# Where the operand rows of a split-float32 decoder trunk lie modulo 256 bytes

## The chip, the cores and the metric

The kernel runs on one core of a Trainium2 chip. The metric is device time in microseconds, the median of several runs. TensorE is called PE for matmuls and PEld for weight loads, VectorE DVE, ScalarE ACT, GpSimd POOL, and the queue that issues the weight transfers SP. SBUF is the on-chip memory that PE reads its operands from; each of its 128 partitions is a row of bytes, and "modulo 256" below speaks of a byte address within such a row.

## The reference, cut to what matters

A trunk of two layers over 256 tokens of width 1024, all in float32:

```python
for l in range(DEPTH):
    h = rms_norm(x, attn_norm[l])
    (c_val, c_gate, n_q, ..., d_q, d_k, d_v) = jnp.split(h @ w_in[l], splits, axis=-1)
    y_a = conv_module(c_val, c_gate, ...)     # gated causal depthwise convolution, 31 taps
    y_b = nsa_mixer(n_q, ...)                 # compressed, selected and windowed attention
    y_c = dilated_mixer(d_q, d_k, d_v, ...)   # three dilations, 12 heads
    x = x + jnp.concatenate([y_a, y_b, y_c], axis=-1) @ w_out[l]
    x = x + conv_ffn(rms_norm(x, ffn_norm[l]), w_up[l], ffn_dw[l], ffn_dw_b[l], w_down[l])
```

The feed-forward part is `u = causal_dwconv(h @ w_up)` (width 5632), then `(silu(gate) * value) @ w_down`.

## The kernel before

**Products of split numbers.** Each float32 operand of a weight product is kept as two rounded parts, hi and lo, and each product is three matmuls: hi by hi, hi by lo, lo by hi (`dense3`, lines 444 to 446). A matmul has a stationary operand of 128 columns, which PEld loads, and a moving operand, which streams through the array. While one matmul streams, the next one's stationary operand is loaded, so PE reads two rows of every partition at once.

**Two kinds of product.** In `feat_block` the weights are loaded and the activations move: 256 columns of `xT_hi` or `xT_lo`, with 128 columns of `whi` or `wlo` stationary. The feed-forward's `up` product (tile name `up`) and the two gated convolution chunks `c0` and `c1` (tile name `cv`) are of this kind. In `tok_chunk` and `proj` it is the other way round: 128 columns of the activations are loaded, and the weights move, 512 columns at a time (tiles `A` and `B` of the attention inputs, `oa` and `ob` of the output product, `da` and `db` of `down`), 384 (`Dq`, `Dk`, `Dv`) or 280 (the smaller chunk of `A`). The first two blocks of `up` in each layer also move the weights, 256 columns at a time (`up_head`, tile name `ut`): on the first of the two token tiles the matmuls with the lo part of the activations stand last (`dense_run`, lines 455, 456, 458), on the second they stand in threes (lines 444 to 446).

**The weight stream.** All weights come in pieces of 128 x 1024 numbers. SP loads a piece into `raw` (4 buffers), ACT writes its rounded part `whi` (line 209), DVE the rest `wlo` (line 212); there are 6 buffers of each and pieces are made 3 ahead of use (`take`, `slots`, `convert_piece`). One piece per layer, the third of `up` (`SPARE_UP`), lies in buffers of the attention stage instead (tile name `sp`).

**Order.** The program is written out in order, and the list `ORDER` interleaves the attention steps with the dilated chunks and the taps of the convolution. In an `up` block (48 matmuls) PE's result is scaled by ACT (line 1027), DVE adds the two other taps (line 222, four instructions), ACT takes the silu, DVE multiplies, and ACT and DVE split the result into `gT_hi` and `gT_lo`, beside two pieces of the weight stream.

**Where the tiles lie.** `cp` (constants and `xT`), `wp` (`raw`, `whi`, `wlo`) and `sp` (small tiles) are pools that lie behind one another in each partition's row; the attention's pool `mp` and the feed-forward's `fp` come behind them. Every slice that a dense product takes begins a whole number of 256 bytes behind its tile's start (the 280-column chunk, whose second half begins 96 bytes further, apart). So one number belongs to each kind of product: the stationary operand's address less the moving one's, modulo 256. The addresses are those which the built program of either kernel gives to its tiles.

| products | moving, stationary | columns | matmuls | distance before | after |
|---|---|---|---|---|---|
| `up` | `xT`, weights | 256 | 1920 | 192 | 64 |
| `cv` | `xT`, weights | 256 | 192 | 192 | 64 |
| `ut` | weights, `xT` | 256 | 192 | 64 | 64 (192 for the 48 that read `sp`) |
| `A`, `B` | weights, `xT` | 512 | 192 | 64 | 0 |
| `Dq`, `Dk`, `Dv` | weights, `xT` | 384 | 576 | 64 | 0 |
| `A`, small chunk | weights, `xT` | 280 | 96 | 64, 224 | 0, 160 |
| `oa`, `ob` | weights, `yT` | 512 | 192 | 192 | 0 |
| `da`, `db` | weights, `gT` | 512 | 528 | 192 | 0 |

Of the kernel before, what the change touches and what calls it, by code (L numbers as in the profile page):

```python
# [12 lines left out]
F32 = mybir.dt.float32  # L13
F32R = mybir.dt.float32r
# [5 lines left out]
P = 128  # L20
# [26 lines left out]
PIECE = 1024  # L47


def piece_list():  # L50
    out = []
    for l in range(L):
        first = ("a0", "a") if l == 0 else ("a", "a0")
        for name in first + tuple(n for n, _ in IN_CHUNKS[2:]):
            cols = CHUNKS[name]
            nk = 4 if len(cols) == 256 else 2
            for h in range(KT // nk):
                out.append((l, name, h, nk * len(cols)))
            if name == "a0":
                out += [(l, "w1", 0, PIECE), (l, "w1", 1, PIECE)]  # L60
        for i in range(KT):
            out.append((l, "out", i, PIECE))
        for f in range(NF):
            out += [(l, "up", 2 * f, PIECE), (l, "up", 2 * f + 1, PIECE)]
        for i in range(NF):
            out.append((l, "down", i, PIECE))
    return out


PIECES = piece_list()  # L70
# [86 lines left out]
W_BUFS = 6  # L157
# [3 lines left out]
SPARE_IN = ()  # L161
ORDER = "np(0) dq(0) t(6) np(1) dk(0) t(6) nf(0) np(2) dv(0) t(6) np(3) nf(1) da(0) dq(1) t(10) dk(1) t(100) ds(1) dv(1) ct(0) pv(1)"
TAIL = 4
CSC = (0,1)
TG = 2
STEP = 8
# [21 lines left out]
def tile_hybrid_trunk(ctx, tc, x_in, pos_in, stream, feats, gains, norms, const_in, out):  # L188
    nc = tc.nc

    cp = ctx.enter_context(tc.tile_pool(name="cp", bufs=1))
    wp = ctx.enter_context(tc.tile_pool(name="wp", bufs=3))
    sp = ctx.enter_context(tc.tile_pool(name="sp", bufs=2))
    ps = ctx.enter_context(tc.tile_pool(name="ps", bufs=1, space=bass.MemoryType.PSUM))

    def mm_bank(nm):
        return ps.tile([P, 512], F32, tag="mm", name=nm, bufs=3)
# [4 lines left out]
    def sc_bank(nm):  # L202
        return ps.tile([P, 1024], F32, tag="sc", name=nm, bufs=1)

    def o_bank(nm):
        return ps.tile([P, 512], F32, tag="o", name=nm, bufs=1)
# [55 lines left out]
    def slots(i):  # L262
        if i in state["spare"]:
            return state["spare"][i](i)
        return [wp.tile([P, PIECE], F32R, tag=t, name=f"{t}{i}", bufs=W_BUFS)[:, :] for t in ("whi", "wlo")]

    def emit_piece():
        i = state["next"]
# [26 lines left out]
    def take(name, ahead=AHEAD):  # L295
        i = cursor["i"]
        assert PIECES[i][1] == name, (PIECES[i], name)
        while state["next"] < min(len(PIECES), i + 1 + ahead):
            emit_piece()
        cursor["i"] += 1  # L300
        return emitted.pop(i)
# [19 lines left out]
    def norm_squares(t, nm, out, split=False):  # L321
        x = x_sb[t]
        ss = sp.tile([P, 2], F32, tag="ss", name=f"ss{nm}", bufs=2)
        for h in range(2):
            sl = slice(h * 512, h * 512 + 512)
            if split and h:
                nc.vector.tensor_tensor_reduce(out=out[:, sl], in0=x[:, sl], in1=x[:, sl], op0=ALU.mult, op1=ALU.add, scale=1.0, scalar=0.0,
                                               accum_out=ss[:, h:h + 1])
            else:
                nc.scalar.activation(out=out[:, sl], in_=x[:, sl], func=AF.Square, accum_out=ss[:, h:h + 1])  # L330
        return ss

    def norm_rms(ss, nm, eng=None):
        a = sp.tile([P, 1], F32, tag="na", name=f"na{nm}", bufs=2)
        ts(a, ss[:, 0:1], ss[:, 1:2], 1.0 / D, ALU.add, ALU.mult, eng=eng)
        ts(a, a, EPS, 1.0, ALU.add, ALU.mult, eng=eng)
        r = sp.tile([P, 1], F32, tag="nr", name=f"nr{nm}", bufs=2)
        rsqrt_into(r, a, [P, 1], nm, eng)
        return r

    def norm_tile(t, gi, nm, r=None):
        x = x_sb[t]
        g = gain_tiles[gi]
        xn = sp.tile([P, D], F32, tag="xn", name=f"xn{nm}", bufs=1)
        if r is None:
            r = norm_rms(norm_squares(t, nm, xn), nm)
        for h in range(2):
            sl = slice(h * 512, h * 512 + 512)
            scaled = stt(xn[:, sl], x[:, sl], r, g[:, sl], ALU.mult, ALU.mult)
            tp = tp_bank(f"tpx{nm}{h}")  # L350
            for k in range(4):
                nc.tensor.transpose(tp[:, k * P:(k + 1) * P], xn[:, h * 512 + k * P:h * 512 + (k + 1) * P], ident)
            tv = tp.rearrange("p (k c) -> p k c", k=4)
            hi = xT_hi[:, h * 4:h * 4 + 4, t * P:(t + 1) * P]
            lo = xT_lo[:, h * 4:h * 4 + 4, t * P:(t + 1) * P]
            ends = copy_act(hi, tv), tt(lo, tv, hi.bitcast(F32), ALU.subtract)
        return ends + (scaled,)
# [8 lines left out]
        )  # L366
    freq = cp.tile([P, 32], F32, name="freq")
    nc.gpsimd.dma_start(freq, const_in[:, CONST_N:CONST_N + 32])
    junk = wp.tile([P, PIECE], F32, tag="whi", name="junk", bufs=W_BUFS)
    ss0 = norm_squares(0, "a00", junk, split=True)  # L370
    x_ready = norm_tile(0, 0, "a00", norm_rms(ss0, "a00"))
    junk = wp.tile([P, PIECE], F32, tag="whi", name="junk1", bufs=W_BUFS)
    ss1 = norm_squares(1, "a01", junk)
    with tc.issue_after(x_ready[2].ins):
        emit_piece()
# [63 lines left out]
    nc.vector.memset(ones_m, 1.0 / 256.0)  # L439
    a_pad = cp.tile([P, 2, S + TAPS - 1], F32, name="a_pad")  # L440
    nc.vector.memset(a_pad, 0.0)

    def dense3(o, a_hi, a_lo, b_hi, b_lo, start, stop):
        nc.tensor.matmul(o, a_hi, b_hi, start=start, stop=False)  # L444
        nc.tensor.matmul(o, a_hi, b_lo, start=False, stop=False)  # L445
        nc.tensor.matmul(o, a_lo, b_hi, start=False, stop=stop)  # L446
# [41 lines left out]
    def feat_block(ws, bank):  # L488
        parts = [split_cols(w, 4) for w in ws]
        for h in range(2):  # L490
            for k in range(KT):
                hi, lo = parts[k // 4]
                sl = slice(h * P, (h + 1) * P)
                dense3(bank[:, h * S:(h + 1) * S], hi[:, k % 4, sl], lo[:, k % 4, sl], xT_hi[:, k, :], xT_lo[:, k, :], k == 0, k == KT - 1)

    for l in range(L):
        f = sp.tile([P, NPF], F32, tag="feat", name=f"feat{l}", bufs=1)
        ff = sp.tile([P, NFF], F32, tag="ffeat", name=f"ffeat{l}", bufs=1)
        ffp = ff.rearrange("p (f h k) -> p f h k", f=NF, h=2)
        c0 = 0  # L500
# [24 lines left out]
        def rope_tables():  # L525
# [3 lines left out]
            for q in Q_ORDER:  # L529
# [10 lines left out]
                ctab[q], stab[q] = c, s  # L540

        def rope(srcs, H, q, slots, nm, dup=False, np_=P):
            n = len(srcs)

# [150 lines left out]
        for b in range(2):  # L695
            ws = [take(f"c{b}") for _ in range(2)]
            bank = sc_bank(f"cv{l}{b}")[:, 0:512] if b in CSC else mm_bank(f"cv{l}{b}")
            feat_block(ws, bank)
# [254 lines left out]
        def proj(name, npieces, kts, a_hi, a_lo, acc, tail):  # L953
            def run(t, w, i, nhs=(0, 1)):
                hi, lo = w
                kk = kts[i]
                for nh in nhs:
                    sl = slice(nh * 512, nh * 512 + 512)
                    dense3(acc[t][nh], a_hi[:, kk, t * P:(t + 1) * P], a_lo[:, kk, t * P:(t + 1) * P], hi[:, sl], lo[:, sl],
                           i == 0, i == npieces - 1)  # L960

            for i in range(npieces - tail):
                w = take(name)
                for t in range(NT):
                    run(t, w, i)
            ws = [take(name) for _ in range(tail)]
            for t in range(NT):
                for nh in range(2):
                    for i in range(tail):
                        run(t, ws[i], npieces - tail + i, (nh,))  # L970
# [5 lines left out]
        obs = [[mm_bank(f"oa{l}{i}") for i in range(2)], [mm_bank(f"ob{l}0"), o_bank(f"ob{l}1")]]  # L976
        proj("out", KT, OUT_ORDER, yT_hi, yT_lo, obs, TAIL)
        for t in range(NT):
# [34 lines left out]
        def up_block(fb):  # L1013
            ws = [take("up") for _ in range(2)]
            bank = mm_bank(f"up{l}{fb}")
            feat_block(ws, bank)
            return bank

        NH = 2
        heads = up_head(NH)  # L1020
        for fb in range(NF):
            bank = heads[fb] if fb < NH else up_block(fb)
            u = fp.tile([P, 2, S], F32, tag="u", name=f"u{l}{fb}", bufs=3)
# [57 lines left out]
```

## Time and profile before

| | |
|---|---|
| median of 3 runs | 754.18 us (752.92 to 754.84) |
| the profiled execution | 753.01 us |
| its span | 751.2 us |
| PE busy | 733.9 us (98%) |
| PEld busy | 639.5 us |
| DVE busy | 597.3 us |
| ACT busy | 487.0 us |
| mean granted PE clock | 0.998 of full speed |
| read from HBM | 117.85 MB |

The busy time of PE is the time covered by at least one matmul record. Records overlap: a matmul's record is 276 to 280 ns long in the `up` stage, while the next one starts some 115 ns later. So what a matmul costs is read from the distance between starts, in the timeline, and not from the mean length of a record.

### The profile page before, as it was taken

How to read it: one execution, taken by the hardware profiler on the slowest of the kernel's cores; microseconds unless marked ns; L12 is line 12 of the kernel's file. 1: busy time of each engine (PE TensorE's matmuls, PEld its weight loads, DVE VectorE, ACT ScalarE, POOL GpSimd, SP SyncE). 2: the span in 40 equal slices, each digit the busy share in tenths (PEclk: the TensorE clock that was granted, in tenths of full speed). 3: DMA queues.
4: the chain of work that ended last, by engine and by line, in shares of the span. 5: the costliest groups of instructions: out<-in, count | busy, mean ns of one | idle time of the engine just before them, and what ended most of it. 6: DMA issues, size and time to landing. Idle time of an engine off the chain costs nothing.

```text
span 751.2 us, 13420 instructions
## 1 busy us (share of the span) xinstructions
PE 733.9 (98%) x4802; PEld 639.5 (85%) x4802; DVE 597.3 (80%) x1377; ACT 487.0 (65%) x1176; POOL 25.5 (3%) x67
## 2 busy tenths in 40 slices
PE   7999999999999999999999999999999999999997
PEld 5788777877999999988878977778789999999885
DVE  6889999886898888854487798989878888888441
ACT  4866998655676666643357589987538666666330
POOL 5200000000000000000040000000000000000000
PEclk9999999999999999999999999999999999999999
DMA  8753224344566555666456241335245656666631
GB/s 319 240 166 117 85 86 133 119 152 142 168 200 194 183 190 190 181 214 187 128 193 230 85 130 41 104 110 188 85 133 177 208 178 191 189 183 196 195 114 57
DMA packets 36005, 119.77 MB, mean 159 GB/s; under 512 B 4113, under 2 KB 4385, under 8 KB 35938
## 3 DMA queue, kind: packets, MB, share of 16 engines
q1 hardware_dynamic: 35714, 118.63, 49.7%
q8 instruction: 38, 0.62, 0.3%
q0 software_dynamic: 224, 0.28, 0.1%
q14 instruction: 29, 0.24, 0.1%
HBM read 117.85 MB, written 1.05 MB: 158 GB/s over the span
## 4 chain that ended last, share of the span: by engine, by line
PE 84%; DVE 6%; ACT 5%; DMA 2%; issue 2%; SPq 0%; DVEq 0%; POOL 0%; ACTq 0%
PE up L445 10%; PE up L444 10%; PE up L446 10%; PE da L444 3%; PE da L446 3%; PE da L445 3%; PE db L444 3%; PE db L446 3%; PE db L445 2%; DVE wlo L212 2%; DMA raw<-in_stream 2%; PE sc L745 1%; ACT whi L209 1%; PE Dk L444 1%; PE Dk L446 1%
## 5 line engine op out<-in xcount | busy, mean ns | idle before, releaser
L212 DVE TENSOR_TENSOR wlo<-raw,whi 128x1024 fp32r<-128x1024 f32 (+3 forms) x232 | 260.3, 1127 | 88.2 <-ACT whi L209 87.3
L209 ACT ACTIVATE whi<-raw 128x1024 fp32r<-128x1024 f32 (+3 forms) x232 | 224.7, 978 | 107.9 <-PE db L446 54.6
L445 PE MATMUL up<-xT_lo,whi 128*128 128x256 f32 x640 | 179.2, 280 | 0.0
L444 PE MATMUL up<-xT_hi,whi 128*128 128x256 f32 x640 | 178.7, 279 | 0.0
L446 PE MATMUL up<-xT_hi,wlo 128*128 128x256 f32 x640 | 178.6, 279 | 0.0
L444 PEld LDWEIGHTS up<-xT_hi,whi 128*128 128x128 f32 x640 | 120.3, 188 | 0.0
L445 PEld LDWEIGHTS up<-xT_lo,whi 128*128 128x128 f32 x640 | 120.1, 188 | 0.0
L446 PEld LDWEIGHTS up<-xT_hi,wlo 128*128 128x128 f32 x640 | 119.7, 187 | 0.0
L222 DVE SCALAR_TENSOR_TENSOR u<-up,ffeat,u 128x255 f32<-128x255 f32 (+1 forms) x176 | 80.0, 478 | 2.6
L222 DVE SCALAR_TENSOR_TENSOR acc<-a_pad,dwh,acc 128x256 f32<-128x256 f32 x120 | 54.2, 480 | 0.3 <-ACT acc L709 0.2
L1034 ACT ACTIVATE sl<-u 128x256 f32<-128x256 f32 x44 | 18.1, 415 | 47.7 <-DVE u L222 47.7
L1027 ACT ACTIVATE u<-up,ffeat 128x256 f32<-128x256 f32 x88 | 44.2, 552 | 0.0
L444 PE MATMUL db<-whi,gT_hi 128*128 128x512 f32 x88 | 34.7, 394 | 0.0
L444 PE MATMUL da<-whi,gT_hi 128*128 128x512 f32 x88 | 34.7, 394 | 0.0
L446 PE MATMUL db<-whi,gT_lo 128*128 128x512 f32 x88 | 34.5, 392 | 0.0
L446 PE MATMUL da<-whi,gT_lo 128*128 128x512 f32 x88 | 34.5, 392 | 0.0
L445 PE MATMUL da<-wlo,gT_hi 128*128 128x512 f32 x88 | 34.2, 388 | 0.0
L445 PE MATMUL db<-wlo,gT_hi 128*128 128x512 f32 x88 | 34.1, 388 | 0.0
L209 ACT ACTIVATE ms<-ms,dd 128x128 f32<-128x128 f32 (+1 forms) x64 | 24.2, 447 | 0.0
L444 PE MATMUL A<-whi,xT_hi 128*128 128x280 f32 (+1 forms) x64 | 23.4, 366 | 0.5 <-ACT xT_hi L209 0.5
L446 PE MATMUL A<-whi,xT_lo 128*128 128x280 f32 (+1 forms) x64 | 22.9, 359 | 0.3 <-DVE xT_lo L212 0.3
L444 PE MATMUL Dq<-whi,xT_hi 128*128 128x384 f32 x64 | 23.0, 359 | 0.0
(348 smaller groups left out, 1573.0 us busy)
## 6 DMA issues: line engine op xcount, KB each, us to landing
raw<-in_stream SPq DMA_DIRECT2D x172, 512.0 KB, 4.2
raw<-in_stream SPq DMA_DIRECT2D x48, 384.0 KB, 3.2
raw<-in_stream SPq DMA_DIRECT2D x8, 280.0 KB, 4.4
w<-in_stream SPq DMA_DIRECT2D x4, 512.0 KB, 5.3
gain<-in_norms SPq DMA_DIRECT2D x3, 512.0 KB, 3.6
x<-in_x SPq DMA_DIRECT2D x4, 256.0 KB, 3.8
out<-x SPq DMA_DIRECT2D x4, 256.0 KB, 2.0
feat<-in_feats SPq DMA_DIRECT2D x2, 339.0 KB, 4.1
```

The source lines that it names most:

```text
L209: return nc.scalar.activation(out=o, in_=i, func=AF.Copy, **kw)
L212: return nc.vector.tensor_tensor(out=o, in0=a, in1=b, op=op)
L222: return nc.vector.scalar_tensor_tensor(out=o, in0=a, scalar=s, in1=b, op0=op0, op1=op1)
L444: nc.tensor.matmul(o, a_hi, b_hi, start=start, stop=False)
L445: nc.tensor.matmul(o, a_hi, b_lo, start=False, stop=False)
L446: nc.tensor.matmul(o, a_lo, b_hi, start=False, stop=stop)
L745: nc.tensor.matmul(sc[:, j * 512:j * 512 + n], QT[hp_, pair, P:2 * P], keys[hp_], start=True, stop=True)
L1027: nc.scalar.activation(out=u[:, h], in_=z, func=AF.Identity, scale=c[:, 2:3], bias=c[:, 3:4])
L1034: nc.scalar.activation(out=sl_, in_=u[:, 0], func=AF.Silu)
```

## The change

The tiles `whi` and `wlo` become 64 numbers (256 bytes) wider, and `slots` gives out 1024 of their columns from a start that depends on the piece: 64 bytes in for `c0`, `c1` and `up`, 192 bytes in for the four pieces of `up` that `up_head` reads (the one in the spare buffers keeps its place there), at the start for all others. Two tiles of 64 bytes, `gap_cp` and `gap_sp`, are put at the end of two pools; they move the pools behind them, so `raw`, `whi` and `wlo` start at 128 modulo 256 in place of 64, and the tiles of `mp` and `fp` (`yT`, `gT` and all else there) lie 128 bytes further. `xT_hi` and `xT_lo` stay at 128. The constant `NH` moves from the function to the top of the file.

```diff
+NH = 2
...
-        return [wp.tile([P, PIECE], F32R, tag=t, name=f"{t}{i}", bufs=W_BUFS)[:, :] for t in ("whi", "wlo")]
+        _, name, h, _ = PIECES[i]
+        at = 16 if name in ("c0", "c1", "up") else 0
+        if name == "up" and h < 2 * NH:
+            at = 48
+        return [wp.tile([P, PIECE + 64], F32R, tag=t, name=f"{t}{i}", bufs=W_BUFS)[:, at:at + PIECE] for t in ("whi", "wlo")]
...
-    junk = wp.tile([P, PIECE], F32, tag="whi", name="junk", bufs=W_BUFS)
+    junk = wp.tile([P, PIECE + 64], F32, tag="whi", name="junk", bufs=W_BUFS)
...
+    for pool in (cp, sp):
+        gap = pool.tile([P, 16], F32, name=f"gap_{pool.name}", bufs=1)
+        nc.vector.memset(gap, 0.0)
```

On all five engines the instructions stand in the same order as before, but for two on DVE. Its first rows before, ahead of the first norm (`junk` holds the squares, `ssa` their sums):

```order
L242 MEMSET one_row 1x128
L439 MEMSET ones_m 128x128
L441 MEMSET a_pad 128x572
L327 ISA junk,ssa_103<-x_67 128x512
L327 ISA ssa_103 128x1
```

and in the changed kernel:

```order
L243 MEMSET one_row 1x128
L444 MEMSET ones_m 128x128
L446 MEMSET a_pad 128x572
L449 MEMSET gap_cp 128x16
L449 MEMSET gap_sp 128x16
L332 ISA junk,ssa_103<-x_67 128x512
```

The two small clears stand between the clear of `a_pad` and the first norm's sum; nothing else moved.

## Rows read from the trace of the kernel before

**Rows 1.** The page, busy us, share of the span and instructions of each engine.

```profile
span 751.2 us, 13420 instructions
...
PE 733.9 (98%) x4802; PEld 639.5 (85%) x4802; DVE 597.3 (80%) x1377; ACT 487.0 (65%) x1176; POOL 25.5 (3%) x67
```

**Rows 2.** The page, the chain that ended last, by engine and line.

```profile
PE 84%; DVE 6%; ACT 5%; DMA 2%; issue 2%; SPq 0%; DVEq 0%; POOL 0%; ACTq 0%
PE up L445 10%; PE up L444 10%; PE up L446 10%; PE da L444 3%; PE da L446 3%; PE da L445 3%; PE db L444 3%; PE db L446 3%; PE db L445 2%; DVE wlo L212 2%; DMA raw<-in_stream 2%; PE sc L745 1%; ACT whi L209 1%; PE Dk L444 1%; PE Dk L446 1%
```

**Rows 3.** Stretches: PE, PEld, DVE, ACT, POOL busy us, clock, DMA share, GB/s.

```profile
60.00:80.00 20.00, 19.66 (x128) 16.54 (x128) 19.89 (x71) 13.83 (x40) 0.00 (x0) 1.00 0.27 81
...
215.00:315.00 100.00, 100.00 (x851) 100.00 (x850) 87.20 (x145) 66.16 (x108) 0.00 (x0) 1.00 0.60 189
```

**Rows 4.** Timeline of PE, up block: start us, us, instruction; 41 starts apart.

```profile
207.12 0.28 PE L444 MATMUL up<-xT_hi,whi 128*128 128x256 f32 x1
...
211.94 0.28 PE L446 MATMUL up<-xT_hi,wlo 128*128 128x256 f32 x1
```

**Rows 5.** Timeline of PE, ut, second token tile, first layer; 44 starts apart.

```profile
196.56 0.28 PE L444 MATMUL ut<-whi,xT_hi 128*128 128x256 f32 x1
...
201.55 0.28 PE L446 MATMUL ut<-whi,xT_lo 128*128 128x256 f32 x1
```

**Rows 6.** Timeline of PE, ut, first token tile, first layer; 9 starts apart.

```profile
189.87 0.28 PE L455 MATMUL ut<-whi,xT_hi 128*128 128x256 f32 x1
...
190.93 0.28 PE L456 MATMUL ut<-wlo,xT_hi 128*128 128x256 f32 x1
```

**Rows 7.** Timeline of PE, ut, first token tile, second layer; 9 starts apart.

```profile
559.36 0.28 PE L455 MATMUL ut<-whi,xT_hi 128*128 128x256 f32 x1
...
560.38 0.28 PE L456 MATMUL ut<-wlo,xT_hi 128*128 128x256 f32 x1
```

**Rows 8.** Timeline of PE, ut, second token tile, second layer; 39 starts apart.

```profile
566.64 0.28 PE L446 MATMUL ut<-whi,xT_lo 128*128 128x256 f32 x1
...
571.06 0.28 PE L446 MATMUL ut<-whi,xT_lo 128*128 128x256 f32 x1
```

**Rows 9.** Timeline of PE, attention input B, 512 columns; 12 starts apart.

```profile
38.64 0.40 PE L444 MATMUL B<-whi,xT_hi 128*128 128x512 f32 x1
...
41.44 0.40 PE L444 MATMUL B<-whi,xT_hi 128*128 128x512 f32 x1
```

**Rows 10.** Timeline of PE, down product, 512 columns; 12 starts apart.

```profile
338.28 0.39 PE L444 MATMUL da<-whi,gT_hi 128*128 128x512 f32 x1
...
341.03 0.39 PE L444 MATMUL da<-whi,gT_hi 128*128 128x512 f32 x1
```

**Rows 11.** Timeline of PE, dilated chunk Dk, 384 columns; 21 starts apart.

```profile
84.22 0.34 PE L444 MATMUL Dk<-whi,xT_hi 128*128 128x384 f32 x1
...
87.93 0.34 PE L444 MATMUL Dk<-whi,xT_hi 128*128 128x384 f32 x1
```

**Rows 12.** Who waited for whom, DVE and ACT, 215 to 315 us: us, times, longest.

```profile
DVE wlo L212 <- ACT whi L209: 9.9, 17, 0.6
...
ACT whi L209 <- PE up L445: 8.4, 17, 1.3
```

**Rows 13.** DVE lines 222 and 439: min/median/max ns, first and last start us, forms.

```profile
L222 DVE SCALAR_TENSOR_TENSOR acc<-a_pad,dwh,acc x120: 473/479/486, 61.5 to 510.6; 128x256 f32<-128x256 f32 x120
...
L439 DVE MEMSET ones_m<- x1: 165/165/165, 1.0 to 1.0; 128x128 f32 x1
```

**Rows 14.** Timeline of DVE, the program's start: clears, then the first norm.

```profile
1.20 0.54 DVE L441 MEMSET a_pad<- 128x572 f32 x1
4.42 0.69 DVE L327 CUSTOM_DVE_ANT_0 junk<-x 128x512 f32<-128x512 f32 x1 [2.69 <-DMA x<-in_x]
```

**Rows 15.** Groups of PE instructions by line and shape: xcount | busy us, mean ns.

```profile
L444 PE MATMUL up<-xT_hi,whi 128*128 128x256 f32 x640 | 178.7, 279 | 0.0
...
L444 PE MATMUL cv<-xT_hi,whi 128*128 128x256 f32 x64 | 18.2, 284 | 0.0
```

More of the change, by code (lines that the diff above doesn't have):

```diff
@@ L368, in tile_hybrid_trunk @@
     nc.gpsimd.dma_start(freq, const_in[:, CONST_N:CONST_N + 32])
-    junk = wp.tile([P, PIECE], F32, tag="whi", name="junk", bufs=W_BUFS)
+    junk = wp.tile([P, PIECE + 64], F32, tag="whi", name="junk", bufs=W_BUFS)
     ss0 = norm_squares(0, "a00", junk, split=True)
     x_ready = norm_tile(0, 0, "a00", norm_rms(ss0, "a00"))
-    junk = wp.tile([P, PIECE], F32, tag="whi", name="junk1", bufs=W_BUFS)
+    junk = wp.tile([P, PIECE + 64], F32, tag="whi", name="junk1", bufs=W_BUFS)
     ss1 = norm_squares(1, "a01", junk)
@@ L1017, in up_block @@
             return bank
-        NH = 2
         heads = up_head(NH)
```

## The prediction

> **What bounds the kernel now.** I read the page first: PE is busy for 733.9 of 751.2 us and no other engine comes near [rows 1]. The chain that ended last goes by PE for 84% of the span, and its three largest entries are the lines of the `up` product, 10% each [rows 2]. In the stretch of `up` from 215 to 315 us PE is covered all the time at a granted clock of 1.00 (the 2.4 GHz level), DVE is busy for 87.20 and ACT for 66.16 of 100 us [rows 3]. So in `up` only the pace of the matmuls counts. Busy time can't show that pace, since records overlap, so the next view is the timeline, and in it the distance between starts.
>
> In `up` 41 starts take 211.94 - 207.12 = 4.82 us, 117.6 ns each [rows 4]. At 2.4 GHz 256 columns would be 106.7 ns, so each matmul loses 10.9 ns although nothing waits. The heads `ut` have the same shape, 256 columns moving against 128 stationary, with the two operands' roles exchanged, and there 44 starts take 4.99 us, 113.4 ns each [rows 5]. What differs is the table's last but one column: distance 192 in `up`, 64 in `ut`. That is the pair of rows that bears on the change.
>
> It isn't clean, and the reader should see that too. On the first token tile `ut` also has distance 64. In the second layer it runs at 1.02 us for 9 starts, 113.3 ns [rows 7], in the first layer at 1.06 us for 9, 117.8 ns [rows 6]. On the second tile of the second layer it is fast again, 4.42 us for 39 starts, 113.3 ns [rows 8]. So distance 64 allows the fast pace and doesn't force it: the stream of loads and the stream of columns settle in one of two rhythms. Of four stretches at distance 64 three are fast; at distance 192 I find the slow one alone.
>
> **The change, part by part.**
>
> *`up`, 192 to 64.* 3 x 640 = 1920 matmuls [rows 15]. If they take the rhythm of [rows 5], each gains 117.6 - 113.4 = 4.2 ns: 1920 x 4.2 = 8.1 us. All of it is on the path, because PE is the only engine in the chain there. The bounds are 0 (rhythm of [rows 6]) and 8.1; I take 8.1, because `up` runs in threes without a break, as [rows 5, 8] do, and those are the nearest rows.
>
> What is late next? A block has 48 matmuls: 48 x 117.6 = 5.64 us now, 5.44 after. DVE needs 87.2% of 5.64, which is 4.92 us, and still fits. Its waits in `up`, 9.9 us in 100, end with ACT's `whi`, and ACT's own wait for a free buffer, 8.4 us, ends with PE [rows 12]; so both shrink when PE is quicker. The transfers use 0.60 of the DMA engines there [rows 3] and would use 0.62.
>
> *`cv`, 192 to 64.* 192 matmuls (three lines of 64 [rows 15]) by 4.2 ns is 0.8 us. DVE is busy for 19.89 of 20 us from 60 to 80 us, where part of them lies [rows 3], so I count half, 0.4 us; the ends are 0 and 0.8.
>
> *Weights that move, to distance 0.* No dense product of the trace has distance 0, so this part is bounded by other rows. 512 columns cost 2.75 us for 12 starts, 229.2 ns, at distance 192 [rows 10], and 2.80 us for 12, 233.3 ns, at distance 64 [rows 9]. The lowest pace seen, 113.4 ns for 256 columns, would be 226.8 ns for 512. For `oa`, `ob`, `da`, `db`, 720 matmuls, the ends are 720 x (226.8 - 229.2) = -1.7 us and 720 x (233.3 - 229.2) = +3.0 us; I take 0, the middle of the three levels. For `A` and `B`, 192 matmuls, the ends are 192 x (226.8 - 233.3) = -1.2 us and one more step of 4.1 ns, +0.8 us; at the middle level they gain 192 x 4.1 = 0.8 us, and I count half, -0.4, as these stages also wait for weights and for ACT. For the 576 matmuls of `Dq`, `Dk`, `Dv`, 3.71 us for 21 starts is 176.7 ns [rows 11]; 1.5 times 113.4 is 170.1, so the ends are 576 x -6.6 = -3.8 us and 576 x 4.1 = +2.4 us. DVE and ACT share the path there, so I take -0.4 us. The 96 matmuls of 280 columns and the 48 of `ut` that read the spare buffers (distance 192, at most +0.2 us) I leave at 0.
>
> *The other engines' operands.* DVE now reads `raw` and `whi` 64 bytes apart where they lay level. The taps of the convolution read `a_pad` at a start that moves by 4 bytes from tap to tap against `acc`; all 120 lie between 473 and 486 ns [rows 13], so I count 0. Were the split of a piece 1% longer, DVE would still have room in `up` by the sum above. ACT and the transfers get no new work, and I count 0.
>
> *The two clears.* 165 ns would be the price of a clear eight times as wide [rows 13]. DVE waits 2.69 us for the first input after its last clear [rows 14], which hides both: 0. Without that cover they would cost 0.3 us.
>
> **Sum.** -8.1 - 0.4 - 0.4 - 0.4 = -9.3 us. The profiled execution took 753.01 us, so one like it would take 743.7 us; it lies 1.2 us under the median of 754.18, and from the median the sum gives **744.9 us**. Each gain is set against the path and I expect none of it to come back in a later stage: `down` is bound by PE as well.
>
> **Rivals.**
>
> *One rhythm of two.* `up` settles in the fast rhythm in one layer and in the slow one in the other, as the first tile of `ut` did [rows 6, 7], or DVE falls behind here and there and gives part of the gain back. Half of `up` remains: 744.9 + 4.1 = 749.0 us. For it: one of four stretches at distance 64 is slow. Against it: in threes, both stretches were fast [rows 5, 8], and a block of `up` doesn't wait for anything that would restart the rhythm.
>
> *The distance has no part in it.* The slow stretch at distance 64 [rows 6] shows that something else sets the rhythm too; if it sets it alone, `up` keeps 117.6 ns and the time is 754 us within a microsecond or two. Against it stands that `up`, 1920 matmuls long, never fell into the fast rhythm. The Trainium skill, "TensorE: Matmul & The Clock Gate", section "Step-by-step: what each phase is for", says that PE has two independent read ports on SBUF, one for the streamed operand and one for the weight load, and that loading the next weights takes no read bandwidth from the running matmul. By that rule the place of the operands could not matter and this rival would hold; by the rows it does matter, since equal shapes run at 113.4 and 117.6 ns.
>
> *Level is the worst place.* The moving weights and the loaded activations now start on the same 256-byte position, and if reads of both rows at once are what costs, level could cost most. The price is in the 720 matmuls of `oa` to `db`, on the path in full: the level of [rows 9] gives +3.0 us, another step in `A`, `B` +0.8, and up to +2.4 in the dilated chunks, 6.2 us together. With the gain of `up` this still leaves 753 us; without it, 760.4 us. It ends on the slower side if `up` gains nothing and the 720 matmuls lose over 3.2 ns each (2.3 us). For it: distance 64 is good at 256 columns and worse than 192 at 512, so the order of places isn't the same for all lengths. Against it: nothing in the trace at distance 0.
>
> **How the numbers follow.** About 0.3%, 2.3 us, is what a measurement of this kernel can tell from no change. Chances: forecast 0.66 (739 to 751 us with the ends of the moving weights), one rhythm of two 0.16 (about 746 to 752), no effect 0.10 (754), level the worst with no gain in `up` 0.08 (757 to 761). The low end of the range is the forecast with all ends on their good side: a further 1.7 + 0.8 + 3.4 + 0.4 = 6.3 us off, 738.6, taken as 739, since not all of the dilated chunks lies on the path. The high end, 752, is one layer's gain with +3.0 us in the 720. Faster by over 0.3% (under 751.9): 0.66 + 0.15 = 0.81; slower: 0.08; within: 0.11.
>
> **What would show it.** Right: starts in `up` 113.4 ns apart, some 880 matmuls in a stretch of 100 us where now there are 851, PE still covered all the time. Starts in `down` between 226.8 and 233.3 ns tell which end holds for level operands; `Dk` between 170 and 181. Wrong: `up` at 117.6 in either layer, a PE that waits for `wlo` in `up`, or `down` beyond 233.3 ns.

## The result, and the profile after

The changed kernel takes **747.24 us**, the median of 20 executions (742.98 to 752.31), against 753.97 us of the kernel before beside it (20 executions, 752.78 to 756.04). The ratio is 0.9907 with a 95% interval of 0.9889 to 0.9926. So it is faster by 0.9%, the sign and the range hold, and the time lies 2.3 us above the forecast of 744.9.

The spread says more than the median. The executions of the kernel before lie within 3.3 us, those of the changed kernel fall into groups: four from 742.98 to 743.38, one at 745.46, twelve from 746.25 to 748.05, three from 751.58 to 752.31. The steps are some 4 us wide, which is what one layer of `up` was worth in the forecast. The granted clock doesn't make the groups: of the fifteen executions with a mean clock of 0.999 or 1.0, four take 742.98 to 743.38, ten 746.62 to 748.05 and one 751.58.

The profiled execution took 752.31 us. Its page, the busy times and the largest entries of the chain (lines have moved: the three matmuls of a dense product are now 452 to 454, the two halves of a split 210 and 213):

```profile
span 750.5 us, 13422 instructions
...
PE 730.9 (97%) x4802; PEld 637.0 (85%) x4802; DVE 597.2 (80%) x1379; ACT 486.9 (65%) x1176; POOL 25.6 (3%) x67
...
PE 84%; DVE 8%; ACT 4%; issue 2%; DMA 2%; SPq 0%; DVEq 0%; ACTq 0%
```

These read like [rows 1, 2]; PE is still the engine that the chain runs through. The difference is in the distance between starts. The timeline of PE, `up` in the first layer, then in the second, 41 starts apart each:

```profile
209.83 0.28 PE L452 MATMUL up<-xT_hi,whi 128*128 128x256 f32 x1
...
214.66 0.28 PE L454 MATMUL up<-xT_hi,wlo 128*128 128x256 f32 x1
...
584.74 0.28 PE L452 MATMUL up<-xT_hi,whi 128*128 128x256 f32 x1
...
589.39 0.28 PE L454 MATMUL up<-xT_hi,wlo 128*128 128x256 f32 x1
```

The first layer needs 4.83 us, 117.8 ns a matmul, as before [rows 4]. The second needs 4.65 us, 113.4 ns, as forecast; over a whole layer the paces are 117.8 and 113.3 ns. Neither changes along the way: from the first dozen starts of a layer to its last block the pace is one of these two. The stretches show the same (PE, PEld, DVE, ACT, POOL busy us, clock, DMA share, GB/s; the row that answers to [rows 3] first, one of the second layer behind it):

```profile
215.00:315.00 100.00, 100.00 (x851) 100.00 (x850) 86.98 (x145) 67.42 (x108) 0.00 (x0) 1.00 0.60 189
...
580.00:680.00 100.00, 100.00 (x885) 100.00 (x884) 90.94 (x153) 70.40 (x114) 0.00 (x0) 1.00 0.63 197
```

851 matmuls in 100 us as before, then 885. PE is covered throughout in both, and DVE rises to 90.94 and still fits.

The moving weights, now level with the activations: `da` (512 columns, 12 starts apart), `B` (512, 12) and `Dk` (384, 17):

```profile
329.79 0.39 PE L453 MATMUL da<-wlo,gT_hi 128*128 128x512 f32 x1
...
332.51 0.39 PE L453 MATMUL da<-wlo,gT_hi 128*128 128x512 f32 x1
```

```profile
41.23 0.39 PE L452 MATMUL B<-whi,xT_hi 128*128 128x512 f32 x1
...
43.96 0.39 PE L452 MATMUL B<-whi,xT_hi 128*128 128x512 f32 x1
```

```profile
87.04 0.33 PE L452 MATMUL Dk<-whi,xT_hi 128*128 128x384 f32 x1
...
89.98 0.33 PE L454 MATMUL Dk<-whi,xT_lo 128*128 128x384 f32 x1
```

`da` takes 226.7 ns a matmul (229.2 in [rows 10]), `B` 227.5 (233.3 in [rows 9]), `Dk` some 173 (176.7 in [rows 11]). The two clears, in the timeline of DVE:

```profile
1.69 0.07 DVE L449 MEMSET gap_cp<- 128x16 f32 x1
1.71 0.07 DVE L449 MEMSET gap_sp<- 128x16 f32 x1
4.41 0.69 DVE L332 CUSTOM_DVE_ANT_0 junk<-x 128x512 f32<-128x512 f32 x1 [2.62 <-DMA x<-in_x]
```

They take 0.07 us each and DVE waits for its input for 2.62 us behind them.

**Why this one execution took 752 us.** With one fast layer it should belong to the 747 group. It lost some 5 us elsewhere: 3.2 us ahead of the first `up` and 2.1 us ahead of the second, against the profile of `after_again` below. Part of that is lost in the first 17 us, at a clock of 1.00: there the first `gain` matmuls start 1.2 us later and the later products of `A` 1.7 us later. The greater part is lost where the granted clock falls, once ahead of each `up`. Stretches of 2 us:

```profile
34.00:36.00 2.00, 0.77 (x5) 0.37 (x4) 1.45 (x4) 1.94 (x5) 1.58 (x4) 1.00 0.89 274
36.00:38.00 2.00, 2.00 (x10) 1.54 (x10) 2.00 (x5) 1.40 (x4) 0.00 (x0) 0.64 0.66 238
38.00:40.00 2.00, 2.00 (x6) 1.61 (x5) 1.10 (x8) 0.64 (x2) 0.00 (x0) 0.50 0.73 244
```

PE is covered for 0.77 of 2 us, a pause inside the product `A` ahead of the small matmuls of `cmp`, and then the granted clock is 0.50 for a while, the 1.2 GHz level. The same pattern stands at 524 to 532 us, behind two shorter pauses. In the profile of `after_again` PE pauses as long and the clock stays:

```profile
32.00:34.00 2.00, 0.77 (x5) 0.28 (x4) 1.50 (x4) 1.95 (x4) 1.94 (x4) 1.00 0.76 223
34.00:36.00 2.00, 2.00 (x11) 1.47 (x12) 2.00 (x4) 1.39 (x4) 0.00 (x0) 1.00 0.69 233
```

What the fall costs is the way from the first matmul of `cmp` to the first of `B`, in the profiled execution and then in `after_again`:

```profile
35.32 0.27 PE L674 MATMUL cmp<-feat,hk 64*32 64x64 f32 x2 [1.23 <-issue]
...
41.23 0.39 PE L452 MATMUL B<-whi,xT_hi 128*128 128x512 f32 x1
```

```profile
33.67 0.27 PE L674 MATMUL cmp<-feat,hk 64*32 64x64 f32 x2 [1.23 <-issue]
...
37.98 0.39 PE L452 MATMUL B<-whi,xT_hi 128*128 128x512 f32 x1
```

That is 5.91 against 4.31 us, so the fall costs 1.6 us here; the one at 528 us costs 1.6 us too, by the same comparison. Such a fall happens in some executions and not in others of the same program, so it isn't set by where the operands lie. The rest is the late start (1.7 us) and 0.5 us at 524 us.

### The profile page after: what moved, and what is told of

Same layout as the page of the kernel before. It is cut to its first block, busy times and chain, and to the rows that moved or that the text cites. A ratio compares the mean times of both kernels' runs of the same rounds, so it can differ in the third digit from the quotient of the medians.

```text
span 750.5 us, 13422 instructions
## 1 busy us (share of the span) xinstructions
PE 730.9 (97%) x4802; PEld 637.0 (85%) x4802; DVE 597.2 (80%) x1379; ACT 486.9 (65%) x1176; POOL 25.6 (3%) x67
## 4 chain that ended last, share of the span: by engine, by line
PE 84%; DVE 8%; ACT 4%; issue 2%; DMA 2%; SPq 0%; DVEq 0%; ACTq 0%
PE up L454 10%; PE up L452 10%; PE up L453 10%; PE da L453 3%; PE da L452 3%; PE da L454 3%; PE db L452 2%; PE db L453 2%; PE db L454 2%; DVE wlo L213 2%; PE sc L753 1%; PE Dk L452 1%; PE Dk L454 1%; PE Dk L453 1%; DMA raw<-in_stream 1%
## 5 line engine op out<-in xcount | busy, mean ns | idle before, releaser
L213 DVE TENSOR_TENSOR wlo<-raw,whi 128x1024 fp32r<-128x1024 f32 (+3 forms) x232 | 260.1, 1126 | 83.1 <-ACT whi L210 82.0
L453 PE MATMUL A<-wlo,xT_hi 128*128 128x280 f32 (+1 forms) x64 | 23.2, 366 | 0.0
```

The source lines that it names most:

```text
L213: return nc.vector.tensor_tensor(out=o, in0=a, in1=b, op=op)
```

## The experiments

Theory: distance decides the pace, and at 64 `up` settles in one of two rhythms when a layer enters it. Rivals: distance has no part; or the whole gain came from the level placement of the moving weights.

**One part alone.** `up_alone` gives the kernel before the distance of 64 in `up` and `cv`, and leaves the moving products at 64 and 192. Against the kernel before (its buffers start 64 bytes further down than those after the change, hence other numbers):

```diff
+        _, name, h, _ = PIECES[i]
+        at = 32 if name in ("c0", "c1", "up") else 0
+        if name == "up" and h < 2 * NH:
+            at = 0
+        return [wp.tile([P, PIECE + 64], F32R, tag=t, name=f"{t}{i}", bufs=W_BUFS)[:, at:at + PIECE] for t in ("whi", "wlo")]
```

> The changed placement for the up and cv products alone: their weights lie 64 bytes behind the activations (distance 64), all other products keep the distances of the kernel before (A, B, Dq, Dk, Dv at 64, oa to db at 192). Theory, two rhythms: each layer's up settles once, at its first matmuls, at 113.4 or at 117.8 ns a start and keeps that to its end, so the times fall into three groups, near 753, 749 and 745 us, and down stays at 229.2 ns. Rival, the distance has no part in it: up at 117.8 ns in both layers of every execution, 754 us within a microsecond. Rival, the gain of the whole change came from the moving weights: no group under 752 us.

`level_alone` does the other half: the changed kernel, with `up` and `cv` back at distance 192.

```diff
-        at = 16 if name in ("c0", "c1", "up") else 0
+        at = 48 if name in ("c0", "c1", "up") else 0
```

> The changed placement for the moving weights alone: A, B, Dq, Dk, Dv, oa to db at distance 0 as in the changed kernel, up and cv at distance 192 as in the kernel before. Theory: up at 117.8 ns a start in every execution, down at 226.7 ns against 229.2, so 720 matmuls gain 2.5 ns each, 1.8 us, and with A and B some 2.5 us in all: 751.5 us in one narrow group. Rival, the spread of the changed kernel comes from the moving weights: times here spread over 8 us as well.

`after_again` is the changed kernel once more beside these two.

> The changed kernel once more, nothing else edited, for a second profile beside a second time. Theory, two rhythms: in each layer all blocks of up run at 113.4 or all at 117.8 ns, and the layer's choice need not be that of the first profile (117.8 in the first layer, 113.3 in the second); an execution with one fast layer takes 747 us, with two 743, with none 751. Rival, the first layer is always slow because of what lies before it: 117.8 there again.

| kernel | median us | all executions | ratio to before, 95% |
|---|---|---|---|
| before | 753.43 | 752.48 to 755.45 | |
| `up_alone` | 749.44 | 745.15, 748.67, 749.04, 749.44, 749.74, 750.0, 752.29 | 0.9937 (0.9913 to 0.996) |
| `level_alone` | 751.78 | 751.27 to 755.31 (12, ten of them up to 753.4) | 0.9981 (0.9969 to 0.9993) |
| `after_again` | 742.86 | 742.21, 742.72, 742.99, 743.85 | 0.9854 (0.9837 to 0.9871) |

Stretches of the two layers of `up`, and 12 starts of the down product, first in `up_alone`:

```profile
215.00:315.00 100.00, 100.00 (x851) 100.00 (x851) 87.29 (x145) 66.51 (x107) 0.00 (x0) 1.00 0.60 190
580.00:680.00 100.00, 100.00 (x884) 100.00 (x884) 90.91 (x151) 69.41 (x113) 0.00 (x0) 1.00 0.65 198
...
329.74 0.39 PE L449 MATMUL db<-whi,gT_hi 128*128 128x512 f32 x1
...
332.49 0.39 PE L449 MATMUL db<-whi,gT_hi 128*128 128x512 f32 x1
```

and in `level_alone`:

```profile
215.00:315.00 100.00, 100.00 (x851) 100.00 (x850) 87.15 (x146) 66.15 (x108) 0.00 (x0) 1.00 0.61 188
580.00:680.00 100.00, 100.00 (x851) 100.00 (x851) 87.59 (x146) 66.53 (x109) 0.00 (x0) 1.00 0.63 191
...
329.72 0.39 PE L452 MATMUL da<-whi,gT_hi 128*128 128x512 f32 x1
...
332.44 0.39 PE L452 MATMUL da<-whi,gT_hi 128*128 128x512 f32 x1
```

At distance 64 one layer is fast (884 starts in 100 us) and one is not; at 192 neither is. The moving weights gain on their own: 2.72 us against 2.75 us for 12 starts, 226.7 against 229.2 ns, and 1.65 us of the time. So neither rival holds for the whole: without level weights the median still falls by 4.0 us, and without distance 64 it falls by 1.65 us. The times of `up_alone` fall as expected around 745 (one) and 749 us (five); the seventh, 752.29, has a mean clock of 0.994, so its time doesn't tell its group.

In `after_again` both layers are fast, 41 starts in 4.64 and 4.65 us:

```profile
209.84 0.28 PE L452 MATMUL up<-xT_hi,whi 128*128 128x256 f32 x1
...
214.48 0.28 PE L454 MATMUL up<-xT_hi,wlo 128*128 128x256 f32 x1
...
584.75 0.28 PE L453 MATMUL up<-xT_lo,whi 128*128 128x256 f32 x1
...
589.40 0.28 PE L452 MATMUL up<-xT_hi,whi 128*128 128x256 f32 x1
```

The same program as in the profile above, in another execution: the program alone doesn't fix the rhythm of a layer. The stage table takes the first start of each stage from the three traces:

| stage, us | before | after, profiled | `after_again` |
|---|---|---|---|
| to the first `up` | 201.7 | 204.0 | 200.8 |
| `up`, first layer | 114.6 | 114.6 | 110.4 |
| down, first layer | 60.4 | 59.9 | 59.9 |
| to the second `up` | 194.4 | 196.8 | 194.7 |
| `up`, second layer | 114.6 | 110.4 | 110.4 |
| down and the end | 65.4 | 64.8 | 64.8 |
| span | 751.2 | 750.5 | 740.9 |

**All distances in one program.** `sweep` gives every block of `up` another distance, eight of them in steps of 32 bytes, in another order in each layer; pieces of the down product and the dilated chunks get theirs too.

```diff
+        turn = (0, 5, 2, 7, 4, 1, 6, 3) if l == 0 else (6, 4, 2, 0, 7, 5, 3, 1)
...
+        if name == "up":
+            at = 48 if h < 2 * NH else 8 * turn[(h // 2 - NH) % 8]
+        elif name == "down":
+            at = 8 * turn[h % 8]
+        elif name[0] == "d":
+            at = 8 * turn[(2 * h + l) % 8 if name[2] == "0" else (2 * h + 1 - l) % 8]
```

> Distances swept inside one execution: from the third block of up on, each block takes one of the eight distances 0, 32 to 224, in one order in the first layer and another in the second; the pieces of down and of the dilated chunks run through the same eight. Only the starts are of interest, not the total time. Theory: the pace of a block changes at its border with the distance; 192 is always at 117.8 ns, 64 at either pace, and if some distance is at 113.4 in both layers and after different neighbours, that is a place that leaves no choice. For 512 columns 0 is at 226.7, 64 near 233.3, 192 near 229.2. Rival, the pace is set by something else than the distance: no change at the borders, one pace through the layer.

It took 753.66 us. A block has 48 matmuls, so the first start of one block to that of the next is its pace. Blocks at 0, 160 and 64 in the first layer (one row for each block's start), the block at 192 there, and a block at 192 in the second layer:

```profile
247.65 0.29 PE L457 MATMUL up<-xT_hi,whi 128*128 128x256 f32 x1
...
253.41 0.28 PE L457 MATMUL up<-xT_hi,whi 128*128 128x256 f32 x1
...
259.16 0.28 PE L457 MATMUL up<-xT_hi,whi 128*128 128x256 f32 x1
...
264.60 0.28 PE L457 MATMUL up<-xT_hi,whi 128*128 128x256 f32 x1
...
281.56 0.28 PE L457 MATMUL up<-xT_hi,whi 128*128 128x256 f32 x1
...
287.01 0.28 PE L457 MATMUL up<-xT_hi,whi 128*128 128x256 f32 x1
...
617.87 0.28 PE L457 MATMUL up<-xT_hi,whi 128*128 128x256 f32 x1
...
623.52 0.28 PE L457 MATMUL up<-xT_hi,whi 128*128 128x256 f32 x1
```

5.76, 5.75 and 5.44 us for 0, 160 and 64, which is 120.0, 119.8 and 113.3 ns; 5.45 us (113.5 ns) for 192 in the first layer and 5.65 us (117.7 ns) in the second. The pace of all distances, ns a matmul, from the starts in the later part of each block:

| distance | 0 | 32 | 64 | 96 | 128 | 160 | 192 | 224 |
|---|---|---|---|---|---|---|---|---|
| `up`, 256 columns | 120.0 | 118.4 | 113.3 | 117.3 | 118.7 | 119.9 | 113.3 or 117.8 | 116.6 |
| down, 512 columns | 226.7 | 232.7 | 233 to 234 | 233 to 234 | 232 | 233 to 234 | 229 | 233 to 234 |

For 384 columns the longest unbroken stretches give 174 to 175 ns at 0, 173 to 174 at 192 and 173 to 177 at the others, too close together to name a best. So the place alone moves `up` by 5.9% within one program, which the rival without distance doesn't allow; the best place for 256 columns is not the best for 512; and 0, with 160 the worst of these eight for `up`, is the best for the down product. One thing was not expected: 192 ran at 113.3 ns in the first layer, so it knows the fast rhythm too. In the order of the kernel before it was never met: none of the 68 executions of that kernel on record is under 752.14 us, and none of the twelve of `level_alone` under 751.27.

Is it the distance, or the place of one operand alone? For 512 columns the rows tell. Distance 192 gave 229 ns with weights at 64 modulo 256 and `gT` at 0 [rows 10] and with weights at 192 and `gT` at 128 (`sweep`); distance 64 gave 233.3 with weights at 64 and `xT` at 128 [rows 9] and 233 to 234 with weights at 192 and `gT` at 128 (`sweep`). Equal distances have equal paces although the places differ. For `up` no run can tell: `xT` lies at 128 in all of them, so the distance and the weights' own place change together.

By the rule of two independent ports in the Trainium skill, "TensorE: Matmul & The Clock Gate", section "Step-by-step: what each phase is for", all blocks would last equally long; the measured 113.3 to 120.0 ns decide against drawing that from it.

**Both rhythms at one distance.** `sweep_seeds` pairs the blocks: first one at a seed distance, then one at 64 (first layer) or 192 (second).

```diff
+            seed = (0, 8, 24, 32, 40, 56, 4, 28, 12, 52)[f // 2 % 10]
+            at = 48 if f < 0 else seed if f % 2 == 0 else 48 if l else 16
```

> Ten seeds, one to each pair of blocks of up: the first block of a pair takes distance 0, 32, 96, 128, 160, 224, 16, 112, 48, 208, the second 64 in the first layer and 192 in the second. Only starts count. Theory, a border chooses between two rhythms by the phase that the block ahead leaves: behind one seed the choice is always the same, and 64 and 192 both know 113.3 and 117.8 ns; behind 128 and 160, 64 runs at 113.3. Rival, 64 forces the fast rhythm and only its first entry behind the transposes fails: every block at 64 at 113.3, every block at 192 at 117.8.

It took 750.29 us. The first starts around two blocks at 64, the first behind one at 32, the second behind one at 96:

```profile
219.67 0.28 PE L454 MATMUL up<-xT_hi,whi 128*128 128x256 f32 x1
...
225.33 0.28 PE L454 MATMUL up<-xT_hi,whi 128*128 128x256 f32 x1
...
230.96 0.28 PE L454 MATMUL up<-xT_hi,whi 128*128 128x256 f32 x1
...
236.41 0.28 PE L454 MATMUL up<-xT_hi,whi 128*128 128x256 f32 x1
```

5.66 us and 5.45 us for the same 48 matmuls at the same distance. At 64 the fast rhythm came behind 48, 96, 128, 160, 208 and 224, the slow one behind 0, 16, 32 and 112. At 192 it is another list: fast behind 0 and 32, slow behind the other eight. So both distances know both rhythms, and a layer can change its rhythm where the distance changes. The distance of the block ahead doesn't settle which one follows: behind 32, 192 is fast here and in the first layer of `sweep`, and slow in the second layer of `sweep`.

**Forcing the rhythm: a miss.** In `seeded` the first block of a layer behind the heads lies at 128, behind which 64 had been fast every time. `seeded_sp` also gives the piece in the spare buffers, which `ut` reads, distance 64 in place of 192 (the last two lines of the diff).

```diff
+        elif name == "up" and h < 2 * NH + 2:
+            at = 32
...
-                mp.tile([P, 3, 3, P], F32, tag="pT", name=f"sp{i}{u}", bufs=4).rearrange("p a b c -> p (a b c)")[:, :PIECE].bitcast(F32R) for u in range(2)]
+                mp.tile([P, 3, 3, P], F32, tag="pT", name=f"sp{i}{u}", bufs=4).rearrange("p a b c -> p (a b c)")[:, 32:32 + PIECE].bitcast(F32R) for u in range(2)]
```

> The changed kernel with one edit: the third block of up in each layer, the first that feat_block makes, takes distance 128 in place of 64; all later blocks stay at 64. In the sweep every block at 64 that came behind one at 160 or 128 ran at 113.3 ns. Theory, the first matmuls choose the rhythm and a border chooses it anew: that block runs at 118.8 ns and all 19 later ones at 113.3 in both layers of every execution; one narrow group of times near 743.5 us (the fast group, 743.0, plus 96 matmuls at 5.4 ns, 0.5 us). Rival, the rhythm drifts or flips by itself in the course of a layer: a spread from 743 to 752 us as with the changed kernel.

> The kernel before this one, and the spare buffers' piece of up begins 128 bytes further in its tile, so that the 48 matmuls of ut that read it have distance 64 like the other 144. Theory: ut no longer drops to 117.8 ns at its second block; at most 96 matmuls gain 4.4 ns, 0.4 us, against seeded; 743.1 us, not to be told from seeded in a few runs. Rival, the first norm's transposes and not ut set the pace there: the same time to 0.1 us.

`seeded`: 743.8, 743.81, 745.73, 748.4, 749.37, 750.5, median 747.06, ratio 0.99 (0.987 to 0.993). `seeded_sp`: 745.52, 745.81, 748.71, 749.21, 751.05, 751.9, median 748.96, ratio 0.9932 (0.9905 to 0.9959). In both profiles all blocks at 64 are fast in both layers, and still the times spread as before, from 743.8 to 748.7 us at a mean clock of 0.999 or more. So a seed that worked in one program does not fix the rhythm of all executions, although the slow ones among these have no trace. The block at 128 itself ran at 120.0 ns in three of the four layers and at 118.6 in one, where 118.8 was expected.

**A distance that comes to the fast rhythm by itself.** `sweep_fine` steps through 24 to 100 by 4 bytes in a shuffled order, reversed in the second layer.

```diff
+        turn = (14, 9, 12, 11, 21, 22, 8, 18, 6, 7, 19, 16, 25, 15, 20, 17, 10, 23, 24, 13)
...
+            at = 48 if f < 0 else turn[f] if l == 0 else turn[19 - f]
```

> Distances 24 to 100 in steps of 4 bytes, one to each block of up, in a shuffled order in the first layer and in the reverse order in the second. Only starts count. Theory, what costs is the overlap of two reads within a 64-byte piece of the row: pace changes smoothly with the distance, 64 is at or near the least, and the same distance has the same pace in both layers but for those with two rhythms. Rival, only multiples of 64 bytes matter: all distances from 36 to 92 but 64 show one common pace.

It took 752.65 us. Block starts at 76 and then 64 in the first layer:

```profile
261.39 0.28 PE L454 MATMUL up<-xT_hi,whi 128*128 128x256 f32 x1
...
266.83 0.28 PE L454 MATMUL up<-xT_hi,whi 128*128 128x256 f32 x1
...
272.27 0.28 PE L454 MATMUL up<-xT_hi,whi 128*128 128x256 f32 x1
```

5.44 us each. Three distances ran at 113.3 ns in both layers: 52, 76 and 88. 64 ran at 113.3 in the first and 117.8 in the second layer. All sixteen others lay between 116.7 and some 122 ns, with no slope: 48 at 117.8 and 56 at 118 stand on either side of 52. The second layer is the better witness: there 52 stood right at the entry, 76 behind a slow 64, 88 behind 32. Both readings of the expectation fall: the pace doesn't change smoothly with the distance, and the distances between the multiples of 64 have no common pace.

`up52`, `up76` and `up88` are the changed kernel with one number altered, 13, 19 or 22; `up52_again` repeats the first.

```diff
-        at = 16 if name in ("c0", "c1", "up") else 0
+        at = 13 if name in ("c0", "c1", "up") else 0
```

> The changed kernel with distance 52 in place of 64 for up and cv, nothing else edited. In the fine sweep 52 ran at 113.3 ns in both layers, once directly behind the transposes. Theory A, 52 has only the fast rhythm: one narrow group near 743 us. Theory B, 52 has a slow rhythm as well, which two looks did not meet: groups at 743, 747 and 751 us as with the changed kernel. Theory C, the sweep's blocks were fast by what stood before them: slow in most executions, above 749 us.

> The changed kernel with distance 76 in place of 64 for up and cv, nothing else edited. In the fine sweep 76 ran at 113.3 ns in both layers, behind 28 and behind 64 in its slow rhythm. Theory A: only the fast rhythm, one narrow group near 743 us. Theory B: two rhythms, groups at 743, 747 and 751 us. Theory C: above 749 us.

> The changed kernel with distance 88 in place of 64 for up and cv, nothing else edited. In the fine sweep 88 ran at 113.3 ns in both layers, behind 84 and behind 32. Theory A: only the fast rhythm, one narrow group near 743 us. Theory B: two rhythms, groups at 743, 747 and 751 us. Theory C: above 749 us.

> The kernel of the run before, up and cv at distance 52, once more and on whatever chip comes. Theory (at 52 the matmuls of up come into the 113.3 ns rhythm from any entry, in both layers of every execution): all times between 742 and 745.5 us, none near 747 or 751, ratio 0.984 to 0.989; in the profile both layers at 113.3 ns. Rival (52 knows both rhythms as 64 does, and four executions were luck): some of the times at 746 to 748.5, one layer at 117.8 ns, or at 751 to 753, both.

| kernel | all executions, us | median | ratio to before, 95% |
|---|---|---|---|
| `up52` | 742.39, 742.98, 742.99, 743.86 | 742.99 | 0.9864 (0.9847 to 0.9881) |
| `up52_again` | 742.54, 743.01, 743.34, 744.82, 746.6 | 743.34 | 0.9872 (0.9849 to 0.9895) |
| `up76` | 742.36, 742.76, 744.84, 745.15, 745.17 | 744.84 | 0.9877 (0.9858 to 0.9896) |
| `up88` | 743.29, 743.35, 743.61, 744.5, 745.2, 749.01 | 744.05 | 0.9886 (0.9861 to 0.9912) |

In each of the four profiles both layers are fast. `up52_again`, 41 starts in each layer, 4.64 and 4.65 us:

```profile
209.83 0.28 PE L452 MATMUL up<-xT_hi,whi 128*128 128x256 f32 x1
...
214.47 0.28 PE L454 MATMUL up<-xT_hi,wlo 128*128 128x256 f32 x1
...
584.82 0.28 PE L452 MATMUL up<-xT_hi,whi 128*128 128x256 f32 x1
...
589.47 0.28 PE L454 MATMUL up<-xT_hi,wlo 128*128 128x256 f32 x1
```

The 745.17 of `up76` is a profiled execution, with both layers fast and a mean clock of 0.91 from 20 to 40 us; of the 2.2 us that its span is longer than that of `up52`, 1.6 us arise in that stretch, so most of the step to 745 is the clock. `up88` at 749.01 (mean clock 1.0) and `up52_again` at 746.6 (0.998) have no trace. The expectation that no execution of `up52_again` would pass 745.5 failed by one of five. At 52 seven of nine executions take under 744 us, where the changed kernel had four of twenty, but a distance that knows only the fast rhythm has not been shown. Nor is 52 shown to be better than 64: it never ran beside the changed kernel, whose four executions in `after_again` were as fast (median 742.86).

## Why the prediction was right, and where it was off

**The price of a matmul in `up`: right.** Forecast 117.6 to 113.4 ns; measured 117.8 to 113.3 [against rows 4, 5]. A layer at the fast pace takes 110.4 us in place of 114.6 in the stage table, 4.2 us each, where the sum had 8.1 for two.

**The term of `up`: the step that failed.** The prediction took the whole 8.1 us "because `up` runs in threes without a break, as [rows 5, 8] do, and those are the nearest rows". Running in threes without a break does not force the rhythm. The slow stretch of [rows 6] was the warning: it lay at the same distance, and the first layer of the profiled execution did just that, at 117.8 ns, which is the sign that the prediction itself named for being wrong ("`up` at 117.6 in either layer"). With one layer of two, the middle group of the executions, the term is 4.2. The rival "one rhythm of two" had the mechanism, with a chance of only 0.16; its own time, 749.0, is 1.8 us over the median, mostly for the next point.

**`down`: counted at 0, worth 1.1 us.** For `oa` to `db` the forecast took the middle of -1.7 and +3.0 us. The rows after show the good end for `down`: 528 matmuls gain 2.2 to 2.5 ns each, and the two stages of `down` in the stage table gain 1.1 us (60.4 to 59.9 and 65.4 to 64.8). For `oa` and `ob` no such gain is seen: from the first matmul of `out` to the first of `ut` the first layer takes 35.50 us before and 35.46 in `after_again`.

**`cv`, `A`, `B` and the dilated chunks: half of what was counted.** The sum had 1.2 us for them. Between the first starts of `B`, `cv`, `Dq` and `oa` in the two traces (before against `after_again`), `B` to `cv` gains 0.26 and 0.17 us in the two layers, `cv` to `Dq` 0.10 and 0.06, `Dq` to `oa` -0.04 and 0.10, together 0.65 us. So the dilated chunks gave next to nothing of their 0.4, although `Dk` itself is quicker; DVE and ACT share the path there, as the prediction said. `A` can't be told apart from the start of the program, which differs by up to 1.7 us between executions.

**Where luck comes in.** The misses together, 744.9 + 4.1 - 1.1 + 0.6 = 748.5 us, come within 1.3 us of the measured median. But 744.9 itself lies between two groups, and the median is that of the middle group, into which twelve of these twenty executions fell. In `after_again` all four fell into the fastest and the median was 742.86. So that the median lies within 2.3 us of the forecast comes from this mixture, which the forecast did not have.

**What is late next: right.** DVE at 4.92 of 5.44 us is 90.4%; the fast layer shows 90.94 of 100, PE covered, and a DMA share of 0.63 (forecast 0.62). The waits of `wlo` and `whi` in such a stretch fall from 9.9 and 8.4 to 5.5 us each. The clears cost nothing behind a wait of 2.62 us. The pace of the splits did not change either: the mean of `wlo` is 1126 ns.

**The rivals.** "The distance has no part in it" falls by `sweep`, where the place moves the pace from 113.3 to 120.0 ns in one program. The two paces that the prediction set against it (113.4 and 117.6 ns) could not decide, since both stood at distance 64 as well [rows 5, 6]. It was right in one thing: something else sets the rhythm too. "Level is the worst place" is true of 256 columns (120.0 ns, the slowest of eight) and false where the change uses it: at 512 columns level is the best of eight. Its 753 us with the gain of `up` was a slip: 754.18 - 8.1 - 0.4 + 6.2 is 751.9.

**What stays open.** What in a layer's entry picks the rhythm isn't settled. The two profiles of the changed kernel show (slow, fast) and (fast, fast), that of `up_alone` (slow, fast). The groups of times fit none, one and two fast layers, but only profiled executions show their layers; for the others this is argued from their times. Why 52, 76 and 88 work and their neighbours don't isn't known, nor why distance matters at all.

## What to carry to other kernels

Where matmuls follow each other without a wait, read the distance between their starts, stage by stage and layer by layer, and compare it with the same shape elsewhere in the trace: a few ns on 2000 matmuls are a per cent that busy time doesn't show. If the pace depends on where the operands lie, sweep the place inside one program, separately for each shape, before choosing one. A single stretch at a pace shows that it can be had, not that every execution has it; where rows at one setting disagree, count the gain once per place where the rhythm is chosen, and look at the spread of the executions as well as at the median.

## What was not expected of the hardware

- A run of 960 matmuls of 256 columns has two steady paces at the same operand places, 113.3 and 117.8 ns. It settles within some dozen starts and then stays for over 100 us, and two executions of one program can differ in it (the profiled execution and `after_again`).
- The pace depends on the distance of the two operands modulo 256 bytes without any order that the runs show: 113.3 ns at 52, 76 and 88, at 64 that or 117.8, 116.7 to some 122 at all other distances from 24 to 100 in steps of 4 (`sweep_fine`).
- 512 columns and 256 columns want different places: 226.7 ns at 0 where 256 columns have 120.0, and 233 to 234 at 64 where they have 113.3 (`sweep`).
- After a pause in which PE was covered for 0.77 of 2 us the granted clock went to 0.50 (1.2 GHz) for some 3 us in one execution, which cost 1.6 us, and stayed at 1.00 in another.
